# Forgetting attention's queries and keys as float16 pairs with a common scale, in a two-layer decoder trunk

## The chip, the cores and the metric

The kernel runs on one core of a Trainium2 chip. The metric is the device time of one execution in microseconds (us). Engines are named as the profile names them: PE (TensorE's products), PEld (its weight loads), DVE (VectorE), ACT (ScalarE), POOL (GpSimd) and SP (SyncE, from whose queue the kernel before starts all its transfers).

## The reference, cut to what matters

Two layers over x of 1024 tokens by 1024 features, float32. Layer 0 mixes by causal pooling and by attention over 256 memory tokens. Between the layers one projection gives the keys, values and forget gates that layer 1 uses. Layer 1 is forgetting attention with 16 heads of 64, and memory attention with 4 heads of 128:

```
h = x @ w_kv_shared                      # keys | values | forget logits
cum = cumsum(log_sigmoid(f_logit), axis=1)
...
logits = einsum('bqhd,bkhd->bhqk', qi, k) * 64 ** -0.5
logits = logits + (ci[..., :, None] - cum_k[:, :, None, :])     # causal mask, softmax, then times v
...
x = layer_norm(ALPHA * x + y @ w_out)    # per layer; y: main and memory part, each times silu of its gate
```

## The kernel before

All products of float32 numbers are made from split operands. A tile of the stream (`A`), a weight (`w`) and the like is a high part in fp32r, a low part in bfloat16 (what the high part leaves) and a rounded copy in bfloat16; `hi_lo` writes them (ACT, DVE, ACT: lines 162, 163, 164), and three products per operand pair (`three`) are summed in one PSUM bank. `slab` (L193) projects one block of 128 output features over all tokens: 48 products of 512 columns into two banks of 512 tokens, with the two weight pieces loaded into `raw` by SP and split as they are needed. Banks are shared by name: `pj` (2), `L` (3), `T` (2), `O` (1).

The order of PE's instructions is the program's in the attention stages (`manual_schedule`). A scheduler orders the other engines' queues, and each engine and SP's queue then works strictly in that order: an instruction that waits holds all that stand behind it.

The stages that matter here, with their times in the profile:

- Layer 0's output projection (`OutProj.rest`, from 330 us): it loads the norm's factors lng and lnb as broadcasts, then takes the tokens in four pairs of tiles, three groups of input features each (`products`), and normalises (`norm`). The transposes of the normalised rows are spread between later products and become the new stream.
- Layer 1's memory keys (`keys` in `mem_kv`), then the four memory queries, each a `slab` with both halves evacuated by `hi_lo`, each followed by one head's memory values (482 to 535 us), then the memory attention (to 600 us).
- `start_units` (605 to 658 us): the first pair of heads' keys and queries, the first values, the forget gates and their running sums, which go to memory (`cumd`, eight small transfers) and come back as broadcast rows `R` (L758) for each head.
- `fox` (658 to 1096 us): 16 heads, 8 query tiles of 128 each, the longest first. In each step `probs` (L761) makes the tile's logits, two products per bank, one against the keys `kx` and one against `ky`; DVE adds `R` and takes the row's minimum (L781); ACT makes the exponentials; the probabilities become a float16 pair, which SP's transfers transpose (`turn`, L824); five steps later the value products (L833) use them. Between these, PE is filled with projections for the next pairs and gates (`fill.pump`).

A pair's keys and queries are made by `qk_units` (L705). A head has 64 features, and its products contract over 128 rows: 64 rows high part and 64 rows low part. For each of the two heads of a pair there is a tile of the queries, a tile `ks` of the keys (own rows high, other rows low) and a tile `ws` with the two swapped. A product with `ks` gives high times high and low times low, one with `ws` the two mixed terms. All are fp32r. Each half of 512 tokens is evacuated head by head in 64 rows (L712, L713 for keys, L723, L724 for queries, which also get the factor -1/8), and `ws` is made from `ks` by four transfers per pair on SP's queue (L716). Queries need no transfer.

## Time and profile before

| | us |
|---|---|
| median of 3 runs | 1220.35 (1218.44 to 1220.95) |
| profiled execution | 1218.15 |
| its span, first to last instruction | 1216.4 |
| PE busy | 1193.7 (98%) |
| DVE busy | 793.3 (65%) |
| ACT busy | 697.4 (57%) |
| POOL busy | 221.0 (18%) |

The mean granted TensorE clock was 0.997. The page gives the busy time of each engine; its groups list instructions by line, with the count, the busy time in all, the mean of one in ns and the idle time of the engine before them with what ended it. A product's mean holds its way through the array, and products follow each other faster than that, so paces are read from the chain of waits or the timeline, which merge neighbours of a kind: start, duration, line, count. Rows of SPq are transfers as SP starts them: their duration there is the start alone.

### The profile page before, as it was taken

How to read it: one execution, taken by the hardware profiler on the slowest of the kernel's cores; microseconds unless marked ns; L12 is line 12 of the kernel's file. 1: busy time of each engine (PE TensorE's matmuls, PEld its weight loads, DVE VectorE, ACT ScalarE, POOL GpSimd, SP SyncE). 2: the span in 40 equal slices, each digit the busy share in tenths (PEclk: the TensorE clock that was granted, in tenths of full speed). 3: DMA queues.
4: the chain of work that ended last, by engine and by line, in shares of the span. 5: the costliest groups of instructions: out<-in, count | busy, mean ns of one | idle time of the engine just before them, and what ended most of it. 6: DMA issues, size and time to landing. Idle time of an engine off the chain costs nothing. (4 is left out here: it accounts for less than half of the span.)

```text
span 1216.4 us, 20026 instructions
## 1 busy us (share of the span) xinstructions
PE 1193.7 (98%) x7018; PEld 758.7 (62%) x7018; DVE 793.3 (65%) x1853; ACT 697.4 (57%) x1474; POOL 221.0 (18%) x349
## 2 busy tenths in 40 slices
PE   9999999999999998999999999999999999999996
PEld 4566666555555666667686666666666666665553
DVE  7534676475644457357736888878877888874754
ACT  6556774374542345567533777767776777685220
POOL 4000000000000000000002454544444434640000
PEclk9999999999999999999999999999999999999999
DMA  6232553232452333234517879988887989895340
GB/s 229 84 112 95 122 131 139 95 121 88 164 182 104 111 129 116 70 96 109 159 52 181 162 161 194 181 187 172 182 195 159 193 188 229 222 241 195 132 156 36
DMA packets 267414, 178.68 MB, mean 147 GB/s; under 512 B 212272, under 2 KB 225712, under 8 KB 267312
## 3 DMA queue, kind: packets, MB, share of 16 engines
q1 hardware_dynamic: 267312, 177.40, 56.2%
q8 instruction: 55, 0.90, 0.3%
q14 instruction: 47, 0.39, 0.1%
HBM read 94.97 MB, written 22.61 MB: 97 GB/s over the span
## 5 line engine op out<-in xcount | busy, mean ns | idle before, releaser
L214 PE MATMUL pj<-A,w 128*128 128x512 bf16 (+1 forms) x2928 | 684.7, 390 | 3.1 <-DVE B L724 1.6
L214 PEld LDWEIGHTS <-w 128*128 128x128 bf16 x1984 | 182.3, 98 | 223.8 <-issue 23.3
L214 PEld LDWEIGHTS pj<-A,w 128*128 128x128 f32 x976 | 181.1, 189 | 45.8 <-ACT A L162 2.8
L789 ACT ACTIVATE T<-MK,s 128x512 f32<-128x512 f32 x192 | 111.3, 580 | 41.5 <-DVE s L781 23.6
L811 DVE SCALAR_TENSOR_TENSOR P<-T,s,P 128x512 f16<-128x512 f32 x192 | 111.6, 613 | 34.7 <-ACT P L810 33.4
L163 DVE TENSOR_TENSOR w<-raw,w 128x512 bf16<-128x512 f32 x106 | 75.6, 714 | 83.6 <-PE pj L214 51.5
L810 ACT ACTIVATE P<-T,s 128x512 f16<-128x512 f32 x192 | 103.0, 576 | 46.0 <-ACT T L789 20.1
L441 PEld LDWEIGHTS <-T 128*128 128x128 bf16 x736 | 70.7, 98 | 82.9 <-issue 3.7
L191 PE MATMUL L<-B,B 128*128 128x512 f32 (+3 forms) x384 | 105.8, 381 | 2.2 <-DVE s L781 2.1
L686 POOL MEMSET G<- 128x128 f32 x1 | 0.2, 208 | 581.5 <-ACT MK L164 581.5
L191 PEld LDWEIGHTS L<-B,B 128*128 128x128 f32 x384 | 70.8, 189 | 22.9 <-DVE s L781 4.8
L162 ACT CAST w<-raw 128x512 fp32r<-128x512 f32 x106 | 65.9, 621 | 26.6 <-PE pj L214 14.6
L157 POOL TENSOR_SCALAR w<-raw 128x512 fp32r<-128x512 f32 x108 | 67.3, 629 | 65.0 <-PE pj L214 59.7
L781 DVE CUSTOM_DVE_ANT_0 MK<-L,R 128x512 f32<-128x512 f32 (+3 forms) x128 | 72.5, 566 | 8.7 <-PE L L191 6.9
L164 ACT CAST w<-raw 128x512 bf16<-128x512 f32 x106 | 65.7, 620 | 18.9 <-PE pj L214 18.2
L773 POOL TENSOR_SCALAR_AFFINE_SELECT R<-R 128x128 f32<-128x128 f32 x128 | 41.3, 328 | 174.4 <-DVE s L781 129.4
L168 POOL TENSOR_TENSOR w<-raw,w 128x512 bf16<-128x512 f32 x54 | 69.6, 1288 | 18.7 <-PE pj L214 16.2
L163 DVE TENSOR_TENSOR T<-T,T 128x1024 bf16<-128x1024 f32 x23 | 28.0, 1218 | 52.2 <-ACT T L162 36.9
L833 PE MATMUL O<-T,V 128*64 128x128 f16 (+1 forms) x1152 | 57.6, 220 | 2.7 <-DMA T<-P 2.5
L833 PEld LDWEIGHTS <-V 128*64 128x64 f16 (+1 forms) x1152 | 50.2, 104 | 15.2 <-issue 5.7
L162 ACT CAST T<-T 128x1024 fp32r<-128x1024 f32 x23 | 24.1, 1046 | 60.3 <-DMA T<-y1d 33.9
L441 PE MATMUL pj<-B,T 128*128 128x512 bf16 (+1 forms) x192 | 52.6, 383 | 0.0
(230 smaller groups left out, 1699.3 us busy)
## 6 DMA issues: line engine op xcount, KB each, us to landing
raw<-in_win_dram SPq DMA_DIRECT2D x96, 256.0 KB, 2.8
raw<-in_wout_dram SPq DMA_DIRECT2D x40, 256.0 KB, 2.8
B<-B SPq DMA_DIRECT2D x32, 256.0 KB, 4.2
R<-cumd SPq DMA_DIRECT2D x16, 512.0 KB, 5.0
y0d<-Y SPq DMA_DIRECT2D x12, 512.0 KB, 3.1
T<-y0d SPq DMA_DIRECT2D x12, 512.0 KB, 3.8
T<-y1d SPq DMA_DIRECT2D x11, 512.0 KB, 4.9
raw<-in_wmk_dram SPq DMA_DIRECT2D x16, 256.0 KB, 2.6
```

What stands on the lines that cost most here:

```text
L157: nc.gpsimd.tensor_scalar(to, src, 1.0, 1.0, ALU.mult, ALU.mult)
L162: pin(nc.scalar.copy(to.hi, src))
L163: pin(nc.vector.tensor_tensor(to.lo, src, to.hi.bitcast(F32), ALU.subtract))
L168: nc.gpsimd.tensor_tensor(to.lo, src, to.hi.bitcast(F32), ALU.subtract)
L191: nc.tensor.matmul(acc, a, b, start=i == 0, stop=i == len(terms) - 1)
L214: nc.tensor.matmul(accs[n], a[:, k, :], b[:, pc * 4 + k, n * NH : (n + 1) * NH], start=seen[n] == 1, stop=seen[n] == 3 * KT,)
L441: nc.tensor.matmul(accs[a][nh], y, w, start=kt == 8 and i == 0, stop=kt == 7 and i == 2,)
L781: nc.vector.tensor_tensor_reduce(p[:, lo:up], lg, R[:, lo:up], 1.0, top, ALU.add, ALU.min, m[:, n : n + 1])
L789: nc.scalar.activation(e, p[:, lo:up], AF.Exp, bias=top, scale=-1.0, accum_out=sums[:, n, hd % 2, i : i + 1],)
L810: nc.scalar.activation(pair[:, lo:up], e, AF.Copy, scale=r)
L811: nc.vector.scalar_tensor_tensor(pair[:, L + lo : L + up], e, r, pair[:, lo:up], ALU.mult, ALU.subtract)
L833: nc.tensor.matmul(acc[rows, (i % 4) * P : (i % 4) * P + P], v[:, b, 2 * j : 2 * j + (1 if e else 2), :].rearrange("p e d -> p (e d)"), pt ...
```

## The change

Keys and queries of the forgetting attention become float16 pairs, divided by a power of two that bounds them. The bound is a product of two: one of the norm's output (32 times the sum of the greatest absolute values of lng and lnb, `bound_of_norm`, in layer 0's output projection), and one of the weights (the greatest sum of absolute values in a row piece of the key and query weights). For the second, all 32 pieces of these weights are loaded a second time, by POOL's own queue, into four buffers that are free then, and ACT sums their absolute values (`look_ahead`, called every sixth product of the memory queries' slabs); DVE takes the maximum, and two transfers on POOL's queue spread it over the partitions (`spread_bound`, `scales_of`).

In `qk_units` a half of 512 tokens is now evacuated in 128 rows for both heads at once: high part by ACT with the factor, low part by DVE (`halves_out`). The rows of the two heads are then arranged by transfers on SP's queue (`move`), six for the keys and three for the queries of a pair; some of them overwrite rows that an earlier one reads. The logits' reduction multiplies back by a factor from a tile (`unq`) where it multiplied by the number 1.0, and the running sums of the gates are scaled beforehand to match. The unused tile `edge` gives way to the tile of row sums.

```diff
@@ in trunk_kernel
-    edge = const.tile([P, 32], F32, name="edge")
-    nc.vector.memset(edge, 0.0)
+    rowsums = const.tile([P, NPIECES], F32, name="rowsums")
+    to_see = [w[p, pc] for p in range(8) for w in (wk, win[1]) for pc in range(2)]
+    landed, lines = [], []
+
+    def look_ahead(after):
+
+        while lines and to_see and len(landed) < len(lines) - 1:
+            k = NPIECES - len(to_see)
+            r = lines[k % len(lines)]
+            nc.gpsimd.dma_start(r, to_see.pop(0))
+            landed.append((k, r))
+        if landed:
+            k, r = landed.pop(0)
+            with tc.issue_after(after):
+                nc.scalar.activation(r, r, AF.Abs, accum_out=rowsums[:, k : k + 1])
+
+    scales = const.tile([P, 8], F32, name="scales")
+    ex, ew, sq, unq, sqk, nsqk, tmp, tmp2 = (scales[:, k : k + 1] for k in range(8))
+
+    def power_of(to, m, least):
+
+        nc.vector.tensor_scalar(m, m, least, None, ALU.max)
+        nc.vector.tensor_scalar(to.bitcast(I32), m.bitcast(I32), 0x7F800000, None, ALU.bitwise_and)
+
+    def bound_of_norm(gb):
+
+        nc.vector.tensor_reduce(tmp, gb[0], AX.X, ALU.max, apply_absolute_value=True)
+        nc.vector.tensor_reduce(tmp2, gb[1], AX.X, ALU.max, apply_absolute_value=True)
+        nc.vector.tensor_tensor(tmp, tmp, tmp2, ALU.add)
+        nc.vector.tensor_scalar(tmp, tmp, 32.0, None, ALU.mult)
+        power_of(ex, tmp, 2.0 ** -2)
+
+    def spread_bound():
+
+        line = dram.tile([P, 1], F32, name=nm("line"))
+        nc.vector.tensor_reduce(tmp, rowsums, AX.X, ALU.max)
+        nc.gpsimd.dma_start(line, tmp)
+        every = lines[0][:, 0, :]
+        nc.gpsimd.dma_start(every, line.rearrange("p o -> (p o)").partition_broadcast(P))
+        return every
+
+    def scales_of(every):
+
+        nc.vector.tensor_reduce(tmp2, every, AX.X, ALU.max)
+        power_of(ew, tmp2, 2.0 ** -24)
+        nc.vector.tensor_tensor(ew, ew, ex, ALU.mult)
+        nc.vector.reciprocal(sqk, ew)
+        nc.vector.tensor_scalar(nsqk, sqk, -(2.0 ** 8), None, ALU.mult)
+        nc.vector.tensor_scalar(sqk, sqk, 2.0 ** 8, None, ALU.mult)
+        nc.vector.tensor_tensor(unq, ew, ew, ALU.mult)
+        nc.vector.tensor_scalar(unq, unq, 2.0 ** -19, None, ALU.mult)
+        nc.vector.reciprocal(sq, unq)
@@ in slab, after each product
+                    if sum(seen.values()) % 6 == 3:
+                        look_ahead(mm.ins)
@@ in mem_attention: after the memory queries, and at its end
+        every = spread_bound() if l else None
...
+        if l:
+            scales_of(every)
@@ in OutProj.rest, after lng and lnb are loaded
+            if X is not None:
+                bound_of_norm(gb)
@@ in layer 1
+        def qk():
+            two = sb([P, 2, S], "B", 10, F16, in1)
+            return two[:, 0], two[:, 1]
+
+        for _ in range(2):
+            for two in (xy((P, 2, 4, P), F32), sb([P, 2, 4, P], "R", 2, F32, in1)):
+                lines.extend((two[:, 0], two[:, 1]))
@@ in forget_gates
-            nc.vector.tensor_copy(cum, ca[:, :n])
+            nc.vector.tensor_scalar(cum, ca[:, :n], sq, None, ALU.mult)
@@ qk_units
+        low64, high64 = slice(0, 64), slice(64, P)
+
+        def move(*moves):
+            for to, rows, of, old in moves:
+                nc.sync.dma_start(to[rows, :], of[old, :])
+
+        def halves_out(hi, lo, cols, acc, factor):
+            nc.scalar.activation(hi[:, cols], acc, AF.Copy, scale=factor)
+            nc.vector.scalar_tensor_tensor(lo[:, cols], acc, factor, hi[:, cols], ALU.mult, ALU.subtract)
+
         def qk_units(p):
-            halves = (slice(0, 64), slice(64, P)), (slice(64, P), slice(0, 64))
-            ks, ws = ([xy() for _ in range(2)] for _ in range(2))
+            (a, b), (c, d) = qk(), qk()
 
             def k_evac(cols, acc):
-                for t, w, (own, other) in zip(ks, ws, halves):
-                    nc.scalar.copy(t[own, cols], acc[own, :])
-                    nc.vector.tensor_tensor(t[other, cols], acc[own, :], t[own, cols].bitcast(F32), ALU.subtract)
-                    if cols.stop == S:
-                        for to, of in ((own, other), (other, own)):
-                            nc.sync.dma_start(w[to, :].bitcast(F32), t[of, :].bitcast(F32))
+                halves_out(a, b, cols, acc, sqk)
+                if cols.stop == S:
+                    move(
+                        (d, high64, a, high64), (c, low64, b, low64), (c, high64, a, low64), (d, low64, b, high64),
+                        (a, high64, b, low64), (b, low64, d, high64),
+                    )
 
             yield from slab(wk[p], X, k_evac)
-            qs = [xy() for _ in range(2)]
+            (e, f), (g, _) = qk(), qk()
 
             def q_evac(cols, acc):
-                for t, (own, other) in zip(qs, halves):
-                    nc.scalar.activation(t[own, cols], acc[own, :], AF.Copy, scale=-0.125)
-                    nc.vector.scalar_tensor_tensor(
-                        t[other, cols], acc[own, :], -0.125, t[own, cols].bitcast(F32), ALU.mult, ALU.subtract,
-                    )
+                halves_out(e, f, cols, acc, nsqk)
+                if cols.stop == S:
+                    move((g, low64, e, high64), (g, high64, f, high64), (e, high64, f, low64))
 
             yield from slab(win[1, p], X, q_evac)
-            pairs[p] = list(zip(qs, ks, ws))
+            pairs[p] = [(e, a, c), (g, b, d)]
@@ in probs
-                nc.vector.tensor_tensor_reduce(p[:, lo:up], lg, R[:, lo:up], 1.0, top, ALU.add, ALU.min, m[:, n : n + 1])
+                nc.vector.tensor_tensor_reduce(p[:, lo:up], lg, R[:, lo:up], unq, top, ALU.add, ALU.min, m[:, n : n + 1])
```

Three things the diff does not show, from the order of the changed program's instructions. The sums of absolute values are not held to the product beside which the program calls for them: six of the 32 stand on ACT before the last transposes of layer 0 are cast, two among the casts of the memory keys, and 24 among the first three memory queries. The maximum over the spread bound (the first step of `scales_of`) stands on DVE in the third memory query, right ahead of the weights' low parts and of that query's second evacuation. And the last two of the keys' moves and the last of the queries' stand on SP one to five places behind the moves that they wait for.

3 lines of the change are left out of this document (2 added, 1 removed).

## Prediction

> **What bounds the kernel now.** I read the page first, then the busy time by stretches, then the chain that ended last, then the groups with their shapes, and last the timelines of the three places where the change puts something in a queue.
>
> ```profile
> span 1216.4 us, 20026 instructions
> PE 1193.7 (98%) x7018; PEld 758.7 (62%) x7018; DVE 793.3 (65%) x1853; ACT 697.4 (57%) x1474; POOL 221.0 (18%) x349
> ```
> ```profile
> 460.00:480.00 20.00, 16.05 (x111) 12.74 (x110) 17.07 (x37) 12.76 (x29) 0.00 (x0) 0.91 0.31 94
> 680.00:700.00 20.00, 18.75 (x144) 12.70 (x143) 17.21 (x48) 14.51 (x34) 6.39 (x12) 1.00 0.79 147
> ```
>
> TensorE (PE) is the bound nearly everywhere: 98% of the span. The second fence is the busy time by 20 us stretches (PE, weight load, DVE, ACT, POOL, granted clock, DMA share). Between layer 0 and layer 1 (460 to 480) PE is short by 4 us; in the forgetting attention (660 to 1096) it is short by a few tenths to 1.25 us per stretch, with DVE at 17 of 20. So whatever shortens PE's own work there shortens the time, unless PE then waits; and whatever makes PE wait elsewhere lengthens it one for one.
>
> **Part 1, the query-key products on PE.** Their count stays (two per bank, 384 in all); only the type changes, fp32r to float16. The chain gives their pace for 512, 384, 256 and 128 columns, and that of 16-bit products; the groups give the counts and one 128-column float16 group.
>
> ```profile
> 1063.15 0.47 PE L L191 x2
> 1067.11 0.35 PE L L191 x2
> 1070.51 0.23 PE L L191 x2
> 1073.57 0.17 PE L L191 x2
> 1086.49 1.73 PE L L441 x8
> ```
> ```profile
> L191 PE MATMUL L<-B,B 128*128 128x512 f32 x160 | 53.8, 433 | 0.0
> L191 PE MATMUL L<-B,B 128*128 128x384 f32 x96 | 28.5, 378 | 0.6 <-DVE s L781 0.6
> L191 PE MATMUL L<-B,B 128*128 128x256 f32 x96 | 22.0, 310 | 1.6 <-DVE s L781 1.5
> L191 PE MATMUL L<-B,B 128*128 128x128 f32 x32 | 8.3, 342 | 0.0
> L191 PE MATMUL T<-T,MK 128*128 128x128 f16 x288 | 17.4, 219 | 0.0
> ```
>
> 512 columns: 0.235 us now, 1.73/8 = 0.216 at 16 bits, 160 x 0.019 = 3.0 us. 384: 0.175 against 0.162 (by columns), 96 x 0.013 = 1.2. 256: 0.115 against 0.108, 96 x 0.007 = 0.7. 128: 0.085 against 17.4/288 = 0.060, 32 x 0.025 = 0.8. Together **-5.7 us**, all on the path while PE is the bound. The mean of 433 ns in the groups is no price: it holds the latency of a pipelined product.
>
> **Part 2, the evacuations and the logits' reduction.**
>
> ```profile
> L724 DVE SCALAR_TENSOR_TENSOR B<-pj,B 64x512 fp32r<-64x512 f32 x32 | 22.1, 689 | 4.4 <-ACT B L723 3.4
> L723 ACT ACTIVATE B<-pj 64x512 fp32r<-64x512 f32 x32 | 18.8, 586 | 13.7 <-DVE B L724 12.3 <-PE pj L214 1.3
> L810 ACT ACTIVATE P<-T,s 128x512 f16<-128x512 f32 x80 | 53.2, 686 | 34.3 <-ACT T L789 13.4 <-issue 12.1 <-DVE s L802 4.8
> L781 DVE CUSTOM_DVE_ANT_0 MK<-L,R 128x512 f32<-128x512 f32 x64 | 43.7, 683 | 8.2 <-PE L L191 6.9 <-POOL R L773 0.9
> L781 DVE CUSTOM_DVE_ANT_0 MK<-L,R,s 128x512 f32<-128x512 f32 x16 | 12.0, 749 | 1.1 <-DVE s L781 0.9
> ```
> ```profile
> PE O L833 <- DMA T<-P: 2.5, 4, 1.2
> PE pj L214 <- DVE B L724: 1.6, 2, 0.8
> ```
>
> Per half of a pair's queries (or keys, alike) two 64-row operations on each engine become one of 128 rows that takes its scale from a tile: on DVE 64 x 0.689 - 32 x 0.749 (the last row's 512 columns with a factor from a tile) = 20 us less, on ACT 64 x 0.586 - 32 x 0.686 = 15.5 us less. Neither engine is the bound, so this counts only where PE waits for it: a bank is free after about 0.69 + 0.75 instead of 0.59 + 0.69 + 0.69 us, and the 1.6 us that PE waits for L724 go: **-1.5 us**. Against it, the 192 reductions (L781) now take their factor from a tile; the row that has one such operand more is 66 ns longer, 8 to 13 us of DVE in all. That lengthens the way from a head's fourth tile (its last long one) to its transpose by 0.13 us or more, while a quicker PE reaches the value products 5 x 0.05 us sooner. Where these already wait for the transposed tile (2.5 us, first row), a third of a microsecond per head is lost again; with 6 of 16 heads so, **+2 us**.
>
> **Part 3, between the layers.** ACT gets 32 sums of absolutes (Abs) of 128x512 whose data POOL loads. In the changed program's order the first five stand on ACT between a cast of stream A and the weight cast for which PE already waits, and POOL may issue their loads only when PE has read layer 0's last weights.
>
> ```profile
> 462.62 0.59 PE L441 MATMUL pj<-MK,T 128*128 128x512 bf16 x2
> 467.60 0.37 ACT L164 CAST MK<-pj 128x256 bf16<-128x256 f32 x1 [1.16 <-DVE MK L163]
> 470.31 0.62 ACT L162 CAST w<-raw 128x512 fp32r<-128x512 f32 x1
> 470.99 1.44 PE L248 MATMUL pj<-T,w 128*128 128x256 f32 x6 [2.29 <-ACT w L162]
> ```
> ```profile
> raw<-in_wk_dram SPq DMA_DIRECT2D x16, 256.0 KB, 3.7
> L789 ACT ACTIVATION_READ_ACCUMULATOR T<-MK,s 128x1 f32 x192 | 36.5, 190 | 0.2
> ```
>
> The trace has no load issued by POOL. Nearest is a 256 KB load of the same tensor from SP, 3.7 us: from 462.8, when the last row of weights is read, the first lands at 466.5, and ACT stands till then, some half a microsecond. An Abs is a cast's 0.62 us, with the 0.19 us of the reading mostly beside the next: five are 3.1 us. ACT's gap of 1.16 us there takes some of that. I take the weight cast of 470.31, and PE with it, **+2.3 us** late; bounds +0.5 (more gaps take them) and +5 (loads land one behind the other).
>
> The Trainium skill (DMA: Bandwidth & Descriptors, "Anatomy of one DMA — SWDGE (gpsimd) path") fits such a load as 2.0 us plus bytes/436e3, an estimate of 2.6 us, which would make this term +1.2; the same page ("SWDGE vs HWDGE vs iDMA") has GpSimd locked out of its descriptor rings by DVE's two-port operations, which speaks for the upper bound. No run so far shows either.
>
> Earlier, in layer 0's out-projection, the bound of the norm puts a maximum over lnb on DVE ahead of the low part of the first products' input:
>
> ```profile
> 328.06 0.42 SPq L462 DMA_DIRECT2D P<-in_lnb_dram  x1
> 330.64 1.22 DVE L163 TENSOR_TENSOR T<-T,T 128x1024 bf16<-128x1024 f32 x1
> 334.36 1.90 PE L441 MATMUL L<-B,T 128*128 128x512 bf16 x8
> P<-in_lnb_dram SPq DMA_DIRECT2D x2, 512.0 KB, 5.7
> ```
>
> lnb lands at 328.06 + 5.7, about 333.8, and the maximum waits for it on DVE; maximum 1.2 (as many elements as the low part) and low part 1.2 end at 336.2. PE's 16-bit products start at 334.36 and need the low part after four of them, at 335.2: **+0.8 us** (0 to 1.5; lnb landed a little sooner makes it nothing).
>
> **Part 4, the memory queries.** Here an operand's bank must be evacuated just before the next slab. The other 24 Abs fill ACT's gaps, and on DVE the wait for the bound's broadcast stands ahead of one evacuation.
>
> ```profile
> 507.62 0.59 ACT L164 CAST B<-pj 128x512 bf16<-128x512 f32 x1 [0.28 <-DVE B L163]
> 508.75 10.76 PE L214 MATMUL pj<-A,w 128*128 128x512 f32 x48
> 520.21 0.68 DVE L163 TENSOR_TENSOR B<-pj,B 128x512 bf16<-128x512 f32 x1
> 521.07 0.59 ACT L164 CAST B<-pj 128x512 bf16<-128x512 f32 x1
> 521.98 2.31 PE L214 MATMUL pj<-A,w 128*128 128x512 f32 x9
> ```
>
> At 508.75 the bank has been free for 0.54 us; the Abs between push its last cast back by about 1.1: +0.6. The broadcast is two POOL transfers one after the other, at 2.6 to 3.7 us each from about 511.7 on, plus ten small steps: DVE is held to about 520.5 and the evacuation of 520.21 comes 1.3 us late, with 0.3 us to spare: +0.9. Together **+1.5 us** (0 to 4).
>
> At nothing I cost the loads themselves: 32 x 256 KB are 8.4 MB in some 65 us, 129 GB/s beside the 94 of the stretch at 460, whose DMA share is 0.31; without that room the weight loads would land later and the bounds of parts 3 and 4 apply. The factors' other steps are one-column operations half a stage ahead of their use, the running sum of the gates is scaled where it was copied, and a pair takes four B buffers of ten instead of six, for which no wait shows.
>
> **Part 5, the moves on SP's queue.** Per pair 4 moves of 256 KB become 9 of 128 KB, of which three overwrite what an earlier one reads and so wait on SP for its landing, with transposes, weight loads and R behind them.
>
> ```profile
> 648.14 4.83 SPq L700 DMA_DIRECT2D cumd<-G  x8
> 658.57 1.07 PE L191 MATMUL L<-B,B 128*128 128x512 f32 x4
> 661.79 2.62 SPq L716 DMA_DIRECT2D B<-B  x4
> B<-B SPq DMA_DIRECT2D x32, 256.0 KB, 4.2
> ```
>
> Head 0's queries had no move; now the first of theirs is issued behind cumd, at 653.0, lands at about 656.5, and the one that waits for it at 660.0; PE wants head 0 at 658.57: **+1.5 us** (0 to 3.5). Later, 5 more issues per pair are 5 x 0.65 us of SP (2.62/4), and a wait of up to 4 us each. In the changed program's order mostly the transposes of a head's last four, short tiles follow them, which are ready early; the fourth tile's, the last one that a head's long value products need, comes right behind a waiting move in about half the heads: **+2 us** (0 to 10).
>
> **The sum.** -5.7 - 1.5 + 2 + 2.3 + 0.8 + 1.5 + 1.5 + 2 = +2.9 us on the profiled execution's 1218.15 (span 1216.4 and 1.75 around it): 1221.0. The median of the runs before is 1220.35, 2.2 above that execution, so I forecast 1223.2.
>
> **The rivals.** *Faster*: the covers hold. ACT is busy 12.76 of 20 us at 460 to 480, and if the loads land by 466 the first Abs fit its gaps; moves stay behind transposes that nobody awaits. Left are -5.7 - 1.5 and some 3 us of small waits: -4.5, 1216. Against it: PE waits for ACT by name there (2.29 us). *Slower by much*: SP becomes the bound of the attention. Decisive is whether a waiting move holds the fourth tile's transpose by more than 1 us in most of the 16 heads, since PE waits for that tile already; at 0.6 us a head more, +10, 1230. Against it: only four such waits now, 2.5 us. *The clock*: a wait of 2.29 us was followed by 9% less clock in its stretch, 3.6 us at half speed; a wait at 658.57 over 2 us would add 1.8 us. By the Trainium skill (TensorE: Matmul & The Clock Gate, Part 1) it takes an idle window of about 3.4 us, so the wait would cost no clock; the row speaks against leaning on that.
>
> **How the numbers follow.** About 0.2%, 2.4 us, can be told from no change. My forecast's own case (0.60) runs from 1220 to 1227, some 0.2 of it within 2.4 us of before; faster 0.25; SP as the bound, with or without the clock, 0.15. So faster 0.25, same 0.20, slower 0.55; the range 1215.5 to 1230 takes the faster case and most of the slow one.
>
> **What would show it.** Right: query-key products as 16-bit at 0.216 us per 512 columns, PE's wait at 470 longer than 2.29 us and put down to ACT, a wait ahead of head 0, DVE's wait ahead of a maximum over the broadcast. Wrong: no longer wait at 470 or at head 0 (then faster), or waits of PE for T<-P well over 2.5 us (then SP). If 16-bit products do not run at 0.216 us, part 1 fails.

## The result, and the profile after

The changed kernel took 1234.74 us (median of 4 runs, 1233.16 to 1235.23) against 1219.69 (1218.44 to 1220.95) of the kernel before in the same comparison: ratio 1.0126, 95% interval 1.0113 to 1.0139. It is slower by 15 us, where 3 were forecast. The profiled execution has a span of 1232.5 us, 16.1 more than before.

First the page, then the waits of PE (in all, times, longest), of the kernel after:

```profile
span 1232.5 us, 20151 instructions
PE 1192.8 (97%) x7018; PEld 731.6 (59%) x7018; DVE 780.8 (63%) x1837; ACT 699.2 (57%) x1506; POOL 239.4 (19%) x383
```
```profile
PE pj L301 <- DVE w L164: 8.5, 2, 4.5
PE O L905 <- DMA T<-P: 5.3, 6, 2.0
PE L L242 <- ACT P L882: 4.9, 3, 1.8
PE L L242 <- DMA B<-B: 3.4, 1, 3.4
```

Then the busy time by stages, before and after. The stretches are cut where the first product of a stage starts: memory keys, first memory query, first values, head 0's first logits, and the last head's end. Columns: stretch, length, busy PE, PEld, DVE, ACT, POOL, granted clock, DMA share, GB/s.

```profile
463.10:482.10 19.00, 15.05 (x114) 13.08 (x113) 15.21 (x33) 14.65 (x32) 0.00 (x0) 0.91 0.41 125
482.10:604.80 122.70, 122.70 (x795) 81.72 (x793) 71.32 (x167) 77.19 (x192) 0.50 (x2) 1.00 0.39 106
604.80:658.60 53.80, 53.60 (x348) 39.45 (x347) 24.11 (x66) 17.90 (x33) 3.17 (x4) 1.00 0.40 114
658.60:1090.80 432.20, 425.70 (x2881) 279.35 (x2880) 349.35 (x993) 312.30 (x721) 200.64 (x326) 1.00 0.88 190
1090.80:1206.80 116.00, 116.00 (x528) 66.77 (x527) 60.62 (x106) 33.04 (x48) 2.39 (x2) 1.00 0.40 135
```
```profile
463.60:484.80 21.20, 16.00 (x115) 13.84 (x114) 15.44 (x33) 17.92 (x43) 7.82 (x14) 0.84 0.83 282
484.80:617.00 132.20, 126.22 (x793) 82.99 (x793) 72.41 (x177) 91.93 (x244) 11.48 (x22) 0.97 0.51 134
617.00:673.80 56.80, 53.46 (x347) 39.34 (x345) 21.00 (x62) 16.04 (x29) 4.76 (x7) 0.99 0.45 119
673.80:1106.20 432.40, 420.86 (x2881) 250.37 (x2882) 337.51 (x967) 299.15 (x696) 199.06 (x324) 0.99 0.90 192
1106.20:1222.20 116.00, 116.00 (x529) 66.76 (x527) 59.69 (x105) 32.03 (x45) 2.38 (x2) 1.00 0.38 133
```

Row against row: +0.5 up to the memory keys (in the first 50 us, where the change does nothing; from there to the memory keys PE waits in neither kernel), +2.2 between the layers, **+9.5** in the memory queries and the memory attention, **+3.0** up to head 0, +0.2 in the forgetting attention, 0 and +0.7 in the rest: 16.1. The forgetting attention, for which the change was made, is as long as before, though PE is busy there for 4.8 us less.

The +9.5 stands in one place. These rows of the timeline (first POOL, then DVE, then PE) and of the DMA issues (size, us to landing) show it, and the two stretches the clock behind it:

```profile
515.72 0.55 POOL L222 DMA_DIRECT2D line<-scales  x1 [10.65 <-DVE scales L221]
523.56 0.55 POOL L224 DMA_DIRECT2D B<-line  x1 [7.29 <-ACT B L163]
527.35 0.29 DVE L229 TENSOR_REDUCE scales<-B 128x1 f32<-128x128 f32 x1 [8.56 <-DMA B<-line]
528.79 1.29 DVE L164 TENSOR_TENSOR w<-raw,w 128x512 bf16<-128x512 f32 x2
529.54 0.82 PE L301 MATMUL pj<-T,w 128*128 128x256 bf16 x3 [4.53 <-DVE w L164]
```
```profile
B<-line POOLq DMA_DIRECT2D x1, 64.0 KB, 3.8
line<-scales POOLq DMA_DIRECT2D x1, 0.5 KB, 7.2
```
```profile
529.00:534.00 5.00, 3.68 (x10) 2.59 (x11) 3.88 (x11) 2.40 (x5) 0.00 (x0) 0.54 0.53 157
534.00:539.00 5.00, 5.00 (x19) 2.09 (x18) 0.48 (x1) 0.22 (x1) 0.00 (x0) 0.78 0.16 52
```

The bound's 512 bytes are sent at 515.72 and have landed 7.2 us later; only then may the second transfer start, which takes 3.8. The first transfer's bytes need few of its microseconds: by the profile no DMA engine is busy from about 517.5 to 525. DVE stands for 8.56 us ahead of the maximum (L229), with the low parts of the memory values' weights (L164) behind it. PE waits 4.53 us for them, and the clock stays at half from about 529.4 to 536.2. Of the 9.5 us, 6.0 are idle time of PE (132.20 less 126.22) and 3.5 are products that ran longer (126.22 against 122.70).

At head 0 (SP's issues, then PE's wait):

```profile
662.79 3.58 SPq L765 DMA_DIRECT2D cumd<-G  x8
666.47 1.11 SPq L774 DMA_DIRECT2D B<-B  x2
668.41 0.34 SPq L830 DMA_DIRECT2D R<-cumd  x1
668.80 0.47 SPq L774 DMA_DIRECT2D B<-B  x1
673.84 1.87 PE L242 MATMUL L<-B,B 128*128 128x512 f16 x4 [3.38 <-DMA B<-B]
```

The queries' moves stand behind the eight writes of cumd, and the last one, which waits for the first, behind R's 512 KB. It lands 4.9 us after its issue, and PE waits 3.38 us. The writes of cumd themselves left late: their numbers were ready at 659.1 (DVE's copy, L763), but SP's queue held two transposes of V, the last of the keys' moves and a weight load ahead of them, and they went out 3.7 us later. In the kernel before they went out 0.3 us after the copy.

### The profile page after: what moved, and what is told of

Read it like the earlier page. It is cut to its first block, busy times and chain, and to the rows that moved or that the text cites. A ratio compares the mean times of both kernels' runs of the same rounds, so it can differ in the third digit from the quotient of the medians.

```text
span 1232.5 us, 20151 instructions
## 1 busy us (share of the span) xinstructions
PE 1192.8 (97%) x7018; PEld 731.6 (59%) x7018; DVE 780.8 (63%) x1837; ACT 699.2 (57%) x1506; POOL 239.4 (19%) x383
## 5 line engine op out<-in xcount | busy, mean ns | idle before, releaser
L265 PE MATMUL pj<-A,w 128*128 128x512 bf16 (+1 forms) x2928 | 694.3, 393 | 3.6 <-ACT A L163 1.5
L265 PEld LDWEIGHTS <-w 128*128 128x128 bf16 x1984 | 188.0, 98 | 222.2 <-issue 20.1
L164 DVE TENSOR_TENSOR w<-raw,w 128x512 bf16<-128x512 f32 x106 | 75.3, 711 | 82.0 <-PE pj L265 43.8
L195 POOL DMA_DIRECT2D B<-in_wk_dram x16 | 9.0, 561 | 452.9 <-PE T L347 443.6
L242 PE MATMUL L<-B,B 128*128 128x512 f16 (+3 forms) x384 | 84.8, 329 | 9.6 <-ACT P L882 4.9
L853 DVE CUSTOM_DVE_ANT_0 MK<-L,R,scales 128x512 f32<-128x512 f32 (+3 forms) x128 | 80.2, 627 | 17.7 <-PE L L242 15.9
L163 ACT CAST w<-raw 128x512 fp32r<-128x512 f32 x106 | 65.9, 622 | 25.8 <-PE pj L265 13.8
L242 PEld LDWEIGHTS <-B 128*128 128x128 f16 x384 | 34.2, 98 | 53.5 <-issue 14.8
L164 DVE TENSOR_TENSOR T<-T,T 128x1024 bf16<-128x1024 f32 x23 | 28.0, 1218 | 55.4 <-ACT T L163 28.2
L301 PE MATMUL pj<-T,w 128*128 128x256 bf16 (+1 forms) x384 | 48.6, 286 | 9.4 <-DVE w L164 8.5
L163 ACT CAST T<-T 128x1024 fp32r<-128x1024 f32 x23 | 24.1, 1047 | 56.2 <-DMA T<-y1d 27.9
```

The source lines that it names most:

```text
L163: pin(nc.scalar.copy(to.hi, src))
L164: pin(nc.vector.tensor_tensor(to.lo, src, to.hi.bitcast(F32), ALU.subtract))
L242: nc.tensor.matmul(acc, a, b, start=i == 0, stop=i == len(terms) - 1)
L265: mm = nc.tensor.matmul(accs[n], a[:, k, :], b[:, pc * 4 + k, n * NH : (n + 1) * NH], start=seen[n] == 1, stop=seen[n] == 3 * KT,)
L853: nc.vector.tensor_tensor_reduce(p[:, lo:up], lg, R[:, lo:up], unq, top, ALU.add, ALU.min, m[:, n : n + 1])
```

## The experiments

All kernels are the changed one with the edit shown, unless said otherwise; times are medians, with the ratio to the kernel before of the same comparison and its interval. Single runs of a variant spread by 1 to 12 us, in most by 3 to 8, and the profiled execution can lie up to 4.6 us from its median; so a difference of one or two microseconds between stages of two profiles is not shown by them alone.

**1. The wait for the broadcast.**

```diff
-        if l:
-            scales_of(every)
+        with tc.issue_after(gated.ins):        # gated: the last ys * gs of the memory attention
+            scales_of(every) if l else None
```

> The changed kernel with one thing moved: VectorE's first look at the broadcast of the weight bound (the maximum over B, line 229, and the small operations behind it) is issued behind the last gating product of layer 1's memory attention instead of in the midst of the memory queries' splits. All the computation stays. Theory: in the trace of the changed kernel VectorE stands 8.6 us in front of that maximum, TensorE loses 4.7 us at 524.7 and 1.1 us at 530.2 to the low parts behind it and then runs at half clock until 534 or so; all of this goes, some 8 us, to about 1226.7 us. Rival (the loss there is the load of 32 weight pieces and their sums on ScalarE and the DMA engines, and the wait only shows it): under 2 us go, 1233 us or more, with another wait at the same place.

1226.15 us, 1.0052 (1.0037 to 1.0067): 8.6 us less than after. The stage:

```profile
485.50:609.10 123.60, 123.22 (x795) 81.89 (x794) 71.58 (x167) 92.03 (x244) 11.49 (x22) 1.00 0.56 144
```

132.2 has become 123.6, with ScalarE as busy as in the changed kernel (92 us). So the loads and sums are hidden there but for 0.9 us (before: 122.7), and the wait's place alone cost 8.6 us: 5.6 of PE's idle time and 3.0 of longer products. The rival falls. The new place is not quite free. The first evacuation of the forgetting attention's keys needs the scale, whose last step now ends at 611.5, and PE waits for it:

```profile
PE pj L722 <- DVE B L778: 0.8, 1, 0.8
```

**2 and 3. Head 0 and the moves.** Four moves for the queries, none overwriting what another reads; and, by itself, cumd's writes on GpSimd's queue:

```diff
-            (e, f), (g, _) = qk(), qk()
+            (e, f), (g, h) = qk(), qk()
-                    move((g, low64, e, high64), (g, high64, f, high64), (e, high64, f, low64))
+                    move((g, low64, e, low64), (h, low64, e, high64), (g, high64, f, low64), (h, high64, f, high64))
-            pairs[p] = [(e, a, c), (g, b, d)]
+            pairs[p] = [(g, a, c), (h, b, d)]
```
```diff
-                nc.sync.dma_start(cumd[:, i * P : (i + 1) * P], ...)
+                nc.gpsimd.dma_start(cumd[:, i * P : (i + 1) * P], ...)
```

> The changed kernel with the queries' halves moved by four transfers into two fresh tiles, none of which overwrites what another still reads, instead of by three of which the last waits for the first. All the computation stays. Theory: the first product of a pair waits for two transfers one behind the other (3.1 us each) after the evacuation; the waits at 670.1, 768.4, 874.4, 980.8 and 1030.6 us (3.5, 0.8, 1.9, 2.0, 1.6 us, 9.8 us in all) shrink by more than half: about 1229 us, 1227 to 1231. Rival (SP's queue bounds this stage): the eight further transfers delay the transposes, the waits of the value products for T<-P grow from 5.3 us to over 8 us and the time stays within 2 us of 1234.7.

> The changed kernel with the eight writes of the cumulative gates (cumd, line 765) issued from GpSimd's queue instead of SP's. All the computation stays. Theory: these eight issues held SP from 662.4 to 666.4 us and put the last move of head 0's queries behind the load of R; without them the first product of the forgetting stage starts some 3 us earlier, the half clock after it (2.8 us) goes too: about 1229 us, 1228 to 1231. Rival (the rows of R, which landed at 673.4 us, are as late and hold the first reduction): TensorE waits as long, now for VectorE's reductions, 1233 to 1235 us.

Four moves: 1235.47 us, 1.0116 (1.0091 to 1.014), nothing gained. cumd on the other queue: 1230.85, 1.0092 (1.0075 to 1.0109), 3.9 less. PE's waits and the stage of the first, and the stage up to head 0 of the second:

```profile
PE O L905 <- DMA T<-P: 12.4, 9, 3.2
```
```profile
672.50:1106.80 434.30, 419.84 (x2881) 250.31 (x2882) 336.61 (x965) 297.03 (x692) 198.17 (x324) 1.00 0.92 194
```
```profile
618.30:672.10 53.80, 53.35 (x347) 39.33 (x345) 21.01 (x62) 15.23 (x28) 6.97 (x12) 1.00 0.43 112
```

The stretch up to head 0 is 53.8 us again, as long as before: the place in SP's queue was the cause there. In the four-move kernel the first products of a pair hardly wait for moves any longer, but the value products wait for their transposed tiles instead, 12.4 us where it was 5.3. The rival holds: the loss at the borders of pairs is passed on, not removed.

**4. Without the sums.** Experiment 1 with the 32 loads and sums left out:

```diff
-    landed, lines = [], []
+    landed, lines, to_see = [], [], nc.vector.memset(rowsums, 32.0) and []
```

> The kernel of the first run with the 32 loads of weight pieces and their 32 sums left out (the row sums are set to the constant 32 instead, so the scale does not follow the weights). Theory: on top of the first run the wait of ScalarE for the first pieces and its six sums between the layers go, which cost TensorE 3.2 us more between 440 and 520 us than before: 2 to 4 us under the first run, about 1223.5 us. Rival (the stretch between the layers is longer for another reason, such as the order of the transposes' casts): within 1 us of the first run.

1224.41 us, 1.0036 (1.0026 to 1.0046), 1.7 under experiment 1, a little less than forecast, and the two intervals overlap. The stretch between the layers:

```profile
464.40:482.00 17.60, 13.66 (x115) 11.70 (x114) 15.08 (x33) 14.72 (x32) 0.56 (x1) 1.00 0.46 139
```

17.6 us instead of 21.2: the sums' loads and their place on ScalarE do cost there. Not all of the 3.6 is theirs: PE waits 2.28 us here, as in the kernel before, and keeps its full clock, while the same wait before was followed by half clock.

**5 and 6. The moves on GpSimd's queue.** Experiments 1 and 3 with the four moves issued by GpSimd (and the bound's write by SP), and then the keys' six too (the bound's write again by GpSimd):

```diff
-                nc.sync.dma_start(to[rows, :], of[old, :])
+                by.dma_start(to[rows, :], of[old, :])           # by=nc.gpsimd
```

> The changed kernel with the late scale of the first run, the writes of cumd on GpSimd's queue as in the third, and the queries' four moves of the second issued from GpSimd's queue instead of SP's; the 512 bytes of the bound are written from SP's queue instead of GpSimd's. All the computation stays. Theory: at the border of two heads' pairs SP's queue is full (in the second run it issued without a gap from 864.8 to 882 us), so that a wait taken from the first product came back at the transposes (waits for T<-P 12.4 us instead of 5.3); with the queries' moves off SP both fall: the loss of TensorE in the forgetting stage goes from 23 us (first run) to 17 us or less, about 1217 us. Rival (the transfers themselves are late, or GpSimd holds its masks back while it waits for the low halves): the loss stays at 22 to 26 us, 1221 us or more. The write of the bound, issue to landing 7.2 to 10.0 us so far: under 4 us if GpSimd's queue makes it slow, as long as before if its 4-byte elements do.

> The kernel e5_queries_pool with the keys' six moves on GpSimd's queue too, and the write of the bound on GpSimd's queue as in the changed kernel. All the computation stays. Theory (SP is the bound): SP sheds nine issues in each pair, 1 to 2 us under e5, about 1215.5 us. Rival: GpSimd, which waits in order, now waits for the keys' moves that overwrite each other as well, its masks come late, VectorE's reductions with them, 1 to 5 us over e5.

1230.43 us, 1.0088 (1.0072 to 1.0103), and 1251.67, 1.0274 (1.0229 to 1.0319): 8.6 us over the base (1221.79, experiment 8 below), and 21 more. The first still waits 14.3 us for T<-P, so it is not SP's queue alone that holds the transposes. In the second, GpSimd waits in its queue for the keys' halves, its masks of R come late, and PE waits for the reductions, beside 15.9 us for T<-P:

```profile
PE L L242 <- DVE s L853: 12.2, 12, 2.5
```

In 5 the bound's write took 9.8 us from SP's queue: GpSimd's queue is not what makes it slow.

**7. The sums in layer 0's output projection**, on top of 5 (the bound's write by GpSimd), landing in the `raw` tiles, called from `rest` every twelfth product:

```diff
+                    (X is not None and (sp or c != 2) and k % 12 == 7) and look_ahead(self.mm.ins)
```

> The kernel e5_queries_pool with the 32 loads and sums of the bound moved into layer 0's output projection, into the weights' landing tiles, where ScalarE was busy for 50 of 133 us; the write of the bound on GpSimd's queue. All the computation stays. Theory: the stretch between the layers is as short as without the sums (TensorE loses 5.4 us there instead of 9.1): about 1213.5 us, under the kernel before. Rival (ScalarE, waiting in order for the pieces, comes late with the splits of the projection's inputs): TensorE waits in 330 to 463 us, where it lost nothing, 1217 us or more.

1243.38 us, 1.0195 (1.0166 to 1.0225). The stretch between the layers fell to 18.6 us, but the projection paid:

```profile
PE pj L497 <- DVE G L548: 7.4, 2, 4.3
PE L L497 <- ACT T L165: 2.4, 1, 2.4
```

**8. The base: 1 and 3 together.**

> The changed kernel with two parts of the earlier runs together: the late scale, and the writes of cumd on GpSimd's queue. All the computation stays. If the two waits are apart, their savings (8.6 and 3.9 us) add: 1222.2 us. If one only stood in front of the other, no more than the larger: 1226 us. The kernel is also the base of the next three.

1221.79 us, 1.0017 (1.0007 to 1.0027). The savings add, 13.0 of the 15 us, and this is the fastest version with the whole computation, still 2 us over the kernel before. Its profiled execution took 1223.92 us, 2.1 above the median.

**9. The sums spread over the projection**: the base and 7's sums, with ScalarE's sums and splits kept in program order.

```diff
-                hi_lo(ys, src)
+                hi_lo(ys, src, X is not None)
+                    (X is not None and sp > 0 and k % 10 == 7) and look_ahead(self.mm.ins)
-                nc.scalar.activation(r, r, AF.Abs, accum_out=...)
+                tc.keep_in_program_order(nc.scalar.activation(r, r, AF.Abs, accum_out=...))
```

> The base (late scale, cumd on GpSimd's queue) with the 32 loads and sums in layer 0's output projection, from its second pair of tiles on, ScalarE's sums and input splits held in the order in which they are written so that they spread over the stage. All the computation stays. Theory: in the run with the sums in that stage all 32 had been put before the first splits and ScalarE was late there (TensorE lost 2.5, 3.3 and 4.7 us at 341, 368 and 374 us); spread, they cost nothing there and the stretch between the layers loses 5.4 us instead of 9.1: 3 us under the base, about 1219 us, level with the kernel before. Rival (the pieces' transfers, 8 MB, hold the projection's own inputs back): over the base.

1260.44 us, 1.033 (1.0312 to 1.0348), the longest of all:

```profile
PE L L497 <- ACT T L163: 9.4, 7, 5.5
PE T L347 <- DVE s L551: 8.0, 3, 3.8
```

With its order held, ScalarE is late for the input splits (L163); PE also waits 8.0 us for DVE's statistics (L551) and 4.7 for ScalarE's casts behind the transposes. Why the pieces hold it so long there, and whether their transfers do, as the rival has it, stays open; that ScalarE was only 38% busy in that stage did not make the sums free.

**10 and 11. What the transfers cost.** The base without any move (the products read the unmoved halves), and the base with `y1d<-G` taken out of the stage:

```diff
-                nc.sync.dma_start(to[rows, :], of[old, :])
+                pass                                            # pairs[p] = [(e, a, b), (e, a, b)]
```
```diff
-            if c == 0:
-                nc.sync.dma_start(y1d[pr // 4, :, pr % 4, :], o)
+            # the eight places written from ys[pr % 4] in the memory attention: the projection reads other numbers
```

> The base with all moves of queries and keys between partitions left out: the products read the halves where they were written, so the same products run on other halves. Theory (the moves, in SP's queue and in the DMA engines, set the waits of the forgetting stage, for the first products and for T<-P alike): the stage, 430 us in the runs so far against an undisturbed 406.6 us of products, shrinks by 6 us or more, to 1216 us or less in all. Rival (the stage waits for the chain of reductions, exponentials and transposes itself): under 2 us. Besides, three writes to memory one behind the other show the landing of 128 rows of 512, 64 and 4 bytes: if the small elements make the bound's write slow, 2 to 3 us for the first and over 7 for the last.

> The base with the writes of the eight pairs' results (y1d<-G, 512 KB each) taken out of the forgetting stage: other tiles are written to those places in the memory attention instead, so the projection reads other numbers. These writes wait for nothing that the products need, and SP's issue of each is 0.4 us. Theory A (the DMA engines, 88 to 90% busy in this stage, are what the moves and transposes queue for): with 4 MB of 82 gone the waits shrink, 3 to 8 us under the base. Theory B (the order in SP's queue and the two transfers in a chain make the waits, not the engines): within 1.5 us of the base.

1216.90 us, 0.9976 (0.9965 to 0.9987), and 1218.76, 0.9991 (0.9981 to 1.0001): 4.9 and 3.0 us under the base: the first between its theory (6 or more) and its rival (under 2), the second at the lower edge of theory A. The stage, first without the moves, then without the write; the base's row stands under experiment 18 (in these profiles 34 of the stage's 2881 products have no record, so PE's busy time is compared among them only):

```profile
665.40:1089.30 423.90, 415.05 (x2847) 248.93 (x2881) 336.92 (x967) 298.60 (x696) 200.42 (x326) 1.00 0.84 176
```
```profile
662.70:1091.20 428.50, 415.45 (x2847) 248.85 (x2881) 337.36 (x967) 299.34 (x697) 200.47 (x326) 1.00 0.91 187
```

Writes for which no product in the stage waits cost 3 us by being there. Whether by the DMA engines or by SP's queue is not shown. The engines' share fell only from 0.93 to 0.91, and the transposes of the probabilities land 4.1 us after their issue in the median with the writes and without. But in the base SP stands 5.1 us in all at these writes, waiting for their numbers, with all that stands behind them.

**12. The sums behind the memory keys**, on the base: GpSimd first copies numbers of the finished keys into the landing lines.

```diff
+            [nc.gpsimd.tensor_copy(r[:, :, 0:1], mk.hi[:, :, 0:1].bitcast(F32)) for r in lines]
```

> The base (late scale, cumd on GpSimd's queue) with the 32 loads and sums where they were, but not before the memory keys: GpSimd first copies a few numbers of the finished keys into each landing line, so that ScalarE's first sum stands behind the keys' last split instead of ahead of the last transposes' casts. All the computation stays. Theory (six sums and the wait for the first piece ahead of those casts make the stretch between the layers longer, 9.0 us lost instead of 6.5 before and 5.4 without sums): 3 us under the base of 1221.8, about 1219 us, level with the kernel before. Rival (the sums cost ScalarE as much wherever they stand, and the memory queries then wait): within 1 us of the base.

1224.04 us, 1.003 (1.0019 to 1.0041): no gain, 2.2 us over the base. The two stretches:

```profile
464.50:484.30 19.80, 16.34 (x115) 14.24 (x114) 15.37 (x33) 14.80 (x32) 0.00 (x0) 0.83 0.36 120
484.30:611.30 127.00, 123.88 (x795) 81.78 (x793) 71.07 (x167) 95.32 (x255) 20.54 (x44) 1.00 0.67 168
```

Against the base the first fell from 21.6 to 19.8 and the second rose from 123.7: what ScalarE does not do between the layers makes the memory queries wait. That is the rival's mechanism; its size (within 1 us) is exceeded.

**13. The bound's write by itself**: experiment 12 with five more writes of 128 numbers, each read back before the next.

```diff
+        return [(nc.gpsimd.dma_start(t, c0), nc.gpsimd.dma_start(c0, t)) for t in (l2, line, l3[:, 0:1], l2, l3[:, 8:9])] and every
```

> The kernel e12_gate with five more writes of 128 numbers to memory behind the bound's, each read back before the next starts: 512 bytes in one piece to a fresh place, the same to the place of the bound, 4 bytes every 64 to a fresh place, then the first and third places again. For the 7.2 to 10.3 us of the bound's write: if it is the 512 adjacent bytes written by all 16 engines, the first, second and fourth take over 6 us and the third and fifth about 1.7 (as 4 bytes every 512 did); if it is the first touch of a place, the first and third are slow and the others fast; if neither, all take about 1.7 us and the slowness belongs to what is under way at that moment.

It took 1224.29 us. The DMA issues of the five, one by one; the third and the fifth put the numbers 64 bytes apart, the others into 512 adjacent bytes. Then three more writes that experiment 10 also held, of 512, 64 and 4 bytes from each partition, 512 bytes apart:

```profile
l<-B POOLq DMA_DIRECT2D x1, 0.5 KB, 8.3
line<-B POOLq DMA_DIRECT2D x1, 0.5 KB, 7.8
l<-B POOLq DMA_DIRECT2D x1, 0.5 KB, 4.5
l<-B POOLq DMA_DIRECT2D x1, 0.5 KB, 8.9
l<-B POOLq DMA_DIRECT2D x1, 0.5 KB, 1.7
```
```profile
probe<-B POOLq DMA_DIRECT2D x1, 64.0 KB, 1.8
probe<-B POOLq DMA_DIRECT2D x1, 8.0 KB, 1.7
probe<-B POOLq DMA_DIRECT2D x1, 0.5 KB, 1.7
```

All three writes into adjacent bytes took 7.8 to 8.9 us, to lines written for the first time and again; 128 numbers 64 or 512 bytes apart took 1.7 (once 4.5). So it is the adjacency of bytes from 128 partitions, not their smallness or the line's first use. The moment adds something of its own, as the 4.5 shows. Each write was seen once, in one execution.

**14 and 16. Evacuations in 64 rows.** On 12, the halves written straight to their head's tile, six moves and no chain; on the base, the low half written into the other rows as in the kernel before, four moves of 128 KB for the keys and none for the queries (and 17: the same with cumd on SP's queue):

```diff
+            for t, r, o in ((hi, low64, high64), (lo, high64, low64)):
+                nc.scalar.activation(t[r, cols], acc[r], AF.Copy, scale=factor[r])
+                nc.vector.scalar_tensor_tensor(t[o, cols], acc[r], factor[r], t[r, cols], ALU.mult, ALU.subtract)
```

> The kernel e12_gate with the halves written straight into the tile of their head (two evacuations of 64 partitions instead of one of 128, as in the kernel before), so that six moves are left in each pair instead of nine and none waits for another. All the computation stays. Leaving all moves out gave 4.9 us. Theory (the moves' transfers and the chain of two are what is left of the loss in the forgetting stage): 2 to 3 us under e12, about 1216.5 us, under the kernel before. Rival (the doubled evacuations on VectorE and ScalarE, 35 us of their time, come back as waits of the reductions): over e12.

> The base (late scale, cumd on GpSimd's queue) with the halves evacuated head by head in 64 rows as in the kernel before, the low half written straight into the other rows of the same tile: float16 pairs and their scales as in the changed kernel, but four moves of 128 KB for a pair's keys and none for its queries. All the computation stays. Theory: without the nine moves, and with half the bytes of before, the products' 5 us show: 4 to 6 us under the base, about 1217 us, under the kernel before. Rival (the evacuations in 64 rows cost what they cost with six moves, when the stage took 8 us more): 1228 us or more.

> The kernel e16_rows64 with the writes of cumd back on SP's queue, where no move of the queries stands behind them any more. All the computation stays. Theory: head 0's wait was the moves' place behind cumd, so without moves of the queries the place of cumd is worth nothing: within 1 us of e16. Rival (R, which waits for cumd, sets the start of head 0): 2 us or more over or under e16.

1233.49 us, 1.0116 (1.0101 to 1.013); 1227.06, 1.0065 (1.0053 to 1.0078); 1228.13, 1.0072 (1.006 to 1.0085). Both rivals of 64 rows win, that of 16 but for 0.9 us. The evacuations of 14:

```profile
L778 DVE SCALAR_TENSOR_TENSOR B<-pj,scales,B 64x512 f16<-64x512 f32 x64 | 47.8, 747 | 10.9 <-ACT B L777 9.8
```

747 ns where the kernel before took 689 for 64 rows, twice as often as in 128 rows. With fewer moves, and half the bytes of before (16), the time is 5.3 us over the base. By the profiles most of this is not in the forgetting attention, which takes 433.60 us against 431.50. The stretch up to head 0 is 3.7 us longer, because the doubled evacuations of the first keys stand behind the late scale: PE waits 2.3 us for them, not 0.8, and 3.4 us at half clock follow. So that the split on 128 rows is worth more than its moves cost is shown for the whole kernel, not for the attention alone; in 14, where that wait cost no clock, the attention takes 439.6 us against 431.6 in 12. Without moves of the queries the place of cumd matters no longer (17 within 1.1 of 16).

**15. The kernel before without its moves.**

```diff
-                            nc.sync.dma_start(w[to, :].bitcast(F32), t[of, :].bitcast(F32))
+                            pass                                # the products take ks for ws
```

> The kernel before with its four moves of 256 KB per pair left out: the products with the swapped keys read the unswapped ones, the same products on other halves. In the changed kernel's base leaving out the nine moves gave 4.9 us. Theory (the nine moves with their chain and the queries' moves, which are needed at once, cost more than the four of before, which nothing needs at once, and so ate the products' 5 us): 0 to 2 us under the kernel before. Rival (moves cost by their bytes, which are nearly the same in both): 4 to 5 us under it, and the products' gain was lost elsewhere, in the reductions with a factor from a tile.

1215.25 us, 0.9965 (0.9952 to 0.9979), 3.8 less. The moves cost the kernel before nearly what they cost the changed one (4.9): the rival is nearer. By the medians about 1 of the products' 5 us went into the moves, a difference within the noise of the two.

**18. The reduction's factor.** The base with the number 1.0 in the reduction, as before:

```diff
-                nc.vector.tensor_tensor_reduce(p[:, lo:up], lg, R[:, lo:up], unq, top, ...)
+                nc.vector.tensor_tensor_reduce(p[:, lo:up], lg, R[:, lo:up], 1.0, top, ...)
```

> The base (late scale, cumd on GpSimd's queue) with the logits' reduction taking the number 1.0 as its factor again instead of a value from a tile, so the logits are not scaled back and the probabilities are others. Theory (what the reductions lost, 61 ns in each of 192, is what a head's chain of reduction, exponential, halves and transpose is longer by, and half of it or more stands on TensorE's path): 4 to 8 us under the base of 1221.8. Rival (VectorE is busy 81% of this stage and has room, so 11.7 us less of it change little): within 1.5 us of the base.

1220.31 us, 1.0001 (0.9989 to 1.0014), 1.5 under the base: at the rival's edge by the medians, and not clear of noise (the intervals overlap), while its profiled stage is 3.6 us shorter. The base's row, then the experiment's:

```profile
664.30:1095.80 431.50, 416.91 (x2847) 249.87 (x2881) 337.20 (x966) 298.76 (x695) 199.87 (x326) 1.00 0.93 193
```
```profile
663.30:1091.20 427.90, 415.38 (x2847) 249.03 (x2881) 328.93 (x967) 300.47 (x697) 199.69 (x326) 1.00 0.91 196
```

## Why the prediction was wrong

The direction was right, and each place that was named is a place where time went, but for layer 0's projection. 1234.7 lies outside 1215.5 to 1230 because of one term above all.

- **Part 4, the memory queries (+1.5, bounds 0 to 4): the step that failed.** The order was read rightly: DVE waits for the broadcast ahead of what PE needs next, though PE missed the low parts of the memory values' weights before the evacuation that the sum went by. But the two transfers were priced as loads, 2.6 to 3.7 us each, from 511.7 on. The row of the bound's write shows 7.2 us, the second transfer 3.8 with 0.6 between. The stage starts 2.7 us later than before, so DVE was free at 528.8, on the old scale 526.1 and not 520.5: 5.6 us too late, 4.3 of them by the transfers and 1.3 by their later start. PE lost 5.6 us to the wait as idle time and 3.0 to the half clock behind it, which this term did not have. Experiment 1 prices the wait at 8.6 us where 0.9 stood in the sum; experiment 13 shows what makes the write slow. The range was at fault as well: no row before had a write of 4 bytes from each partition, and a landing of 256 KB was taken for its upper end.
- **Part 5, head 0 (+1.5, 0 to 3.5): right in mechanism, mis-sized.** The first move went out behind cumd and the last one behind its landing, as worked out, and the two took 7.2 us (2.3 and 4.9, the last beside R) where 7.0 was put. What was off is the end of cumd's writes: taken 5.6 us ahead of head 0, as in the kernel before, it was 4.1, since the keys' six moves and the transposes of V in SP's queue held them. PE waited 3.38 us, the stretch grew by 3.0, and the clock came on top: the rival of the clock held here. Experiment 3 prices both at 3.9 us.
- **Part 5, later (+2, 0 to 10).** Waits for T<-P rose from 2.5 to 5.3 us. Not foreseen was the other wait, of a pair's first products for the last move; the profile shows it as PE L L242 behind ACT (4.9 us). Experiments 2 and 5 show that a wait taken away at one place returned at the other, and experiment 15 that the moves of before had cost 3.8 us already. Which limit lies behind this, SP's queue, the DMA engines or the chain through DVE and ScalarE, is not shown.
- **Part 1 (-5.7): right.** PE's busy time in the stage fell from 425.70 us to 420.86, and to 420.00 in experiment 3, where the clock was full in that stage.
- **Part 2 (-1.5 and +2): the reductions about right, the evacuations open.** The reductions grew by 55 to 61 ns each; by experiment 18's medians 1.5 us of it reached the end, which is not clear of noise. The evacuations' gain was probably put too low: 64-row evacuations cost 9.4 us in 14, though they are off PE's path by the profile. But they took their factor from a tile there, 747 ns against 689 before, so this is not the price of the kernel before's.
- **Part 3 (+2.3 and +0.8): the first right in size, partly by luck, the second nothing.** Of the +2.2 between the layers, 1.2 are idle time of PE and 1.0 longer products at a lower clock (0.84 against 0.91), which the sum did not have. In layer 0's projection the maximum over lnb stood ahead of the low part, as worked out, but that was done at 335.5, a little after PE's 16-bit products had begun (334.93), and PE did not wait; the 0.5 us were lost in the first 50 us. The chain between the layers was one step longer than written: PE's 4 us wait is put down to DVE's low part, which stood behind stream A's, which waited for casts that stood behind the first sums:

```profile
467.89 0.63 ACT L200 ACTIVATE B<-B 128x512 f32<-128x512 f32 x1 [1.43 <-DMA B<-in_wk_dram]
470.10 1.05 ACT L163 CAST A<-T 128x512 fp32r<-128x512 f32 x2
473.21 1.46 PE L301 MATMUL pj<-T,w 128*128 128x256 bf16 x6 [3.98 <-DVE w L164]
```

Of the 15 us, 13.0 are the two waits (experiment 8). Where the 2 that are left come from is only roughly known. In the base's profile the stretch between the layers is 2.6 us longer than before, the memory queries and the memory attention 1.0, and the forgetting attention only 0.7 shorter (431.50 against 432.20), though its products are some 5 us shorter. Of the rest of that gain the reductions (1.5) and the moves (1) account for about half, by differences of single experiments that are near the noise; the other half has no place yet.

## What to carry to other kernels

A wait in an in-order queue costs by where it stands, not by how late its data is needed: ask first whether what stands behind it has slack, and put it behind the last thing that has none; here the same maximum cost 8.6 us at one place and, 80 us later, 0.8. A transfer whose kind no row of the trace shows has no price yet: measure it alone before a range is built on it, above all a round trip through memory that everything behind it waits for. Where a wait removed at one place shows up at the next, as in experiments 2 and 5, the gain of faster products has to be looked for in the whole stage's length.

## What the runs showed of the hardware

- A write of 512 adjacent bytes to memory, 4 from each of 128 partitions, landed after 7.2 to 11.9 us in all of 18 profiles, 17 times from GpSimd's queue and once from SP's; the same numbers 512 bytes apart landed after 1.7. A 256 KB load that SP had issued 1.6 us ahead of it landed after 7.2 us as well, where its like in the kernel before took 2.6; that the write held it up was not tried by itself. The Trainium skill (DMA: Bandwidth & Descriptors, "Anatomy of one DMA — SWDGE (gpsimd) path") gives 2.0 us and almost nothing for the bytes, which fits the spread write and not the adjacent one; it says as well that the landing is mostly the wait for the memory's receipt, and that fits a write that is under way from 515.7 to 522.9 while the DMA engines are idle from about 517.5.
- GpSimd's loads of 256 KB landed after 5.5 to 6.0 us in the median where thirteen were issued within 12 us between the layers, and the first of them took 3.9. By the fit in the same section of the Trainium skill (DMA: Bandwidth & Descriptors) the estimate is 2.6.
- The clock: waits of 4.53, 3.98 and 3.38 us were each followed by half clock (0.54 and 0.50 in the next five microseconds). In rows of 1 us, half clock lasted either 3.4 or 6.8 us each time: 6.8 at fourteen of fifteen waits of 3.4 to 4.5 us, in twelve profiles, and 3.4 at the other (experiment 1, 4.49 us). Of ten waits of 2.3 us, three cost no clock (experiments 4 and 14, twice there), five cost 3.4 us at half clock (the kernel before, where the row of 19 us shows 9% less, and experiments 7, 13, 16 and 17) and two cost 6.8 (12 and 15). The Trainium skill (TensorE: Matmul & The Clock Gate, Part 1) has an idle window of about 3.4 us that runs freely. That agrees with the long waits, with the two lengths and with the chance in the short ones, though not with its length for the 2.3 us.
